# A hybrid decoder step on one core: differences kept in SBUF, per-layer stores moved to GpSimd

## The chip, the cores and the metric

The kernel runs on one core of a Trainium2 chip. The metric is the device time of one execution in microseconds. Before the change the median of three runs is 2677.23 us (2677.14 to 2685.69).

## The reference, cut to what matters

One decoder layer over 1024 prompt positions and 8 single-step samples, so 1032 columns (`NT`). Two branches (an SSD branch and a gated delta branch) are merged, then come an FFN and per-layer embeddings:

```python
h = _rms_norm(x, norm_mix)
proj = jnp.einsum('bld,de->ble', h, w_in)           # z, xbc, dt, qkv, gate, b, a, mgate
y, new_ssm = _ssd_chunked(...)                       # branch 1
o, new_gdn = _gated_delta_chunked(...)               # branch 2
o = _rms_norm(o, gdn_norm) * jax.nn.silu(gate)
mix = g_ssm * (y @ w_branch_ssm) + g_gdn * (o @ w_branch_gdn)
x = x + mix @ w_out
gt, up = jnp.split(_rms_norm(x, norm_ffn) @ w_ffn_in, 2, axis=-1)
x = x + (jax.nn.silu(gt) * up) @ w_ffn_out
pe = p @ w_pl_proj
x = x + pe * jax.nn.sigmoid(_rms_norm(x, norm_pl) @ w_pl_gate)
return _rms_norm(x, norm_final)
```

All data is float32 in DRAM. The kernel splits each operand into a high and a low part (`fp32r`), and takes three matmuls for a product: high by high, high by low, low by high.

## The kernel before, in words

Columns of x are features on 128 partitions in 8 blocks, rows are positions. The whole residual stays in SBUF as `x2` (also named `acc`). Matmul results lie in eight PSUM tiles of four pools: `pd` (3), `pt` (2), `py` (2), `pz` (1).

A scheduler orders the instructions of each engine by data and priority; weights are loaded by `load_w` with a high priority. `split_raw` splits a weight on ScalarE (`wh`, L138) and VectorE (`wl`, L139). All DMAs of the kernel before are issued from SyncE (`SPq` in rows), in the order in which the scheduler lists them, so a DMA that waits holds those listed behind it.

*The early stage.* `load_o` (L1085) brings the eight blocks of the delta branch: a block of `og_d` and one of the gate, silu on ScalarE, product on VectorE, then the split into `o` (`hilo`, L189 and L190). Blocks 0 to 3 take the two `lt` buffers, 4 to 7 the `op` slab tiles; all gate blocks share the two `sg` buffers. The per-layer inputs `pr` are loaded beside it and transposed into `ple`, which is stored to `ple_d` (L1111). The first two per-layer products `pe` follow, their copies out of PSUM on ScalarE (L1123). Then the eight blocks of the branch product with `o`; `residual` (L1153) loads a block of x into `xf` and transposes it into `x2`.

*The output product* runs in two halves of 516 columns. Behind the second half's blocks 4 to 7 the differences `t3` of two feature blocks are computed and stored to `t3_d` (L1248). Behind the first half, eight normalised tiles `n` are split into `b11` and `b21`, and stored to `n_d`. `roots` makes the inverse root `rb` (reciprocal, L1206).

*The late stage.* The FFN's first product uses a Strassen-like scheme of seven half-size products over row halves: tiles `b11`, `b21`, `bt1` to `bt4` and `b22` are its right sides (names in rows drop the digits: `bq` holds `b11`, `b21`, `bt2` and `bt3`; `t` is `t3`, `n` is `n1` and `n2`, `g`, `u`, `x` are sums). Before it, `per_layer_late` (L1128) makes the other six blocks of `pe` as fillers: 18 products of six matmuls over 344 columns, in six PSUM tiles in turn; ScalarE copies each (L1133) into one of five staging tiles (`x1`, two of `g1`, `u2`, `u3`), from which it is stored to `pe_d` (L1134). While TensorE does these, the block under `prep` reloads `t3` and `n` (L1308 to L1311), and makes the right sides on VectorE: L1318 multiplies `t3` by `rb`, L1319 and L1323 make sums and differences, `put` (L1224 and L1225) splits, L1228 scales again, L1327 makes the rows of `bt1`. Behind all of it stand the two first sums: `ffn_first(0)` and `ffn_first(1)`, each two products of 12 matmuls by two column halves over `b11` and `b21`; the second product's result is added by VectorE (L1284) into `g`. Then `ffn_in(0)` takes the other five products of row 0, each also by two column halves.

Of the kernel before, what the change touches and what calls it, by code (L numbers as in the profile page):

```python
# [8 lines left out]
F32 = mybir.dt.float32  # L9
# [7 lines left out]
P = 128  # L17
# [3 lines left out]
NB = 8  # L21
NT = NP + NB
# [17 lines left out]
def hybrid_step(  # L40
# [9 lines left out]
    V, S, G, TE = nc.vector, nc.scalar, nc.gpsimd, nc.tensor  # L50
    dma = nc.sync.dma_start
# [7 lines left out]
    dr = ctx.enter_context(tc.tile_pool(name="dr", bufs=1, space=DRAM))  # L59
# [12 lines left out]
    ident = cp.tile([P, P], F32, name="ident")  # L72
# [132 lines left out]
    with (  # L205
# [4 lines left out]
        for tt in range(9):  # L210
            n = P if tt < 8 else NB
# [8 lines left out]
        for g in range(3):  # L220
            t0, tn = PARTS[g]
            xns = []
            for tt in range(3 * g, 3 * g + 3):
                n, xt = (P if tt < 8 else NB), xts[tt]
# [7 lines left out]
            for k in range(KD):  # L232
                pool, name = ((pt, "pt"), (py, "py"), (pz, "pz"), (pt, "pt"), (py, "py"))[k % 5]
                t = pool.tile([P, 512], F32, name=name)
# [23 lines left out]
    pe_d = dr.tile([8, P, NT], F32, name="pe_d")  # L258
# [1 line left out]
    vb_d = dr.tile([8, P, NC, P], F32, name="vb_d")  # L260
    ple_d = dr.tile([2, P, 2, NT], F32, name="ple_d")
    n_d = dr.tile([8, P, NT // 2], F32, name="n_d")
    t3_d = dr.tile([4, P, NT // 2], F32, name="t3_d")
    bcd_d = dr.tile([2, 4, NB, P], F32, name="bcd_d")


# [49 lines left out]
    with tc.tile_pool(name="pr", bufs=1, side="right", reuse_waits="tile") as pr:  # L316
# [67 lines left out]
        for hh in range(2):  # L384
            q = slice(64 * hh, 64 * hh + 64)
# [3 lines left out]
        for src, dst in ((acum, colA), (dtb, colB), (q1, colQ)):  # L389
            for q in range(2):  # L390
                t = pt.tile([P, 512], F32, name="pt")
# [249 lines left out]
    with (  # L641
# [35 lines left out]
        def solves():  # L677
            for b4 in range(2):
                yield from solve(b4)
                yield  # L680
# [146 lines left out]
        last, side = None, solves()  # L827
# [248 lines left out]
    pM = ExitStack()  # L1076
    slb = pM.enter_context(tc.tile_pool(name="slb", bufs=8, reuse_waits="tile"))
    b2 = pM.enter_context(tc.tile_pool(name="b2", bufs=2, reuse_waits="tile"))

    def part_tile(name, dt=F32R):  # L1080
        return slb.tile([P, 2, NT], dt, name=name, tag="parts")

    ops = []

    def load_o(dst, k):  # L1085
        if k >= 4 and k % 2 == 0:
            ops.append(part_tile("op", F32))
        t = b2.tile([P, NT], F32, name="lt") if k < 4 else ops[-1][:, k % 2]
        dma(t[:, :NP], og_d[k])
        G.tensor_copy(t[:, NP:], odec[:, k])  # L1090
        gt = b2.tile([P, NT], F32, name="sg")
        dma(gt, gate_d[k])
        S.activation(gt, gt, AF.Silu)
        V.tensor_tensor(t, t, gt, ALU.mult)
        hilo(dst[:, 0, k % 4], dst[:, 1, k % 4], t)

    pacts = []
    for k in range(2):
        t = part_tile("ple")
        pacts.append((t[:, 0], t[:, 1], t))  # L1100
    for tt in range(9):
        n = P if tt < 8 else NB
        pr_ = b2.tile([P, 256], F32, name="pr", tag="xf")
        dma(pr_[:n], p_prompt[0, 0, tt * P : tt * P + P, :] if tt < 8 else p_sample[0, :, 0, :])
        t = pt.tile([P, 512], F32, name="pt")
        ts = slice(tt * P, tt * P + n)
        for k in range(2):
            TE.transpose(t[:, k * P : k * P + n], pr_[:n, k * P : k * P + P], ident[:n, :n])
            hilo(pacts[k][0][:, ts], pacts[k][1][:, ts], t[:, k * P : k * P + n])
# [18 lines left out]
    def per_layer_late(f, pacts, pools, rooms):  # L1128
        def ev(t0, tn, o):
            pool, name = rooms[0]  # L1130
            rooms.append(rooms.pop(0))
            t = pool.tile([P, NT // 2], F32, name=name, bufs=2 if name == "g1" else 1)
            S.copy(t[:, :tn], o)  # L1133
            dma(pe_d[f, :, t0 : t0 + tn], t[:, :tn])  # L1134

        dense(load_w(w_pl_proj[:, f * P : f * P + P], 2), pacts, ev, CHUNKS, pools)

# [13 lines left out]
    x2 = acc  # L1151

    def residual(f):  # L1153
        xf = b2.tile([P, 9, P], F32, name="xf")
        fs = slice(f * P, f * P + P)
        dma(xf[:, 0:8], x_prompt[0, :, fs].rearrange("(t p) d -> p t d", p=P))
        dma(xf[:NB, 8], x_sample[:, 0, fs])
        for q in range(3):
            t = pt.tile([P, 512], F32, name="pt")
            n = 4 if q < 2 else 1  # L1160
            w = P if q < 2 else NB
            for k in range(n):
                TE.transpose(t[:, k * P : k * P + w], xf[:w, 4 * q + k], ident[:w, :w])
            S.copy(x2[:, f, 512 * q : 512 * q + n * w], t[:, : n * w])

    macts = []
# [1 line left out]
    for f in range(8):  # L1168
# [4 lines left out]
        sg = sgp[f][:, 1] if f < 2 else b2.tile([P, NT], F32, name="sg")  # L1173
# [38 lines left out]
    QT = NT // 2  # L1212
# [10 lines left out]
    def put(q, k, src):  # L1223
        S.copy(q[:, 0, k], src)  # L1224
        V.tensor_tensor(q[:, 1, k], src, q[:, 0, k].bitcast(F32), ALU.subtract)  # L1225

    def scaled(dst, j, ts):
        V.scalar_tensor_tensor(dst, x2[:, j, ts], gain(G_FFN, j), rb[:, ts], ALU.mult, ALU.mult)  # L1228

    for hf in range(2):  # L1230
        parts = tuple((hf * QT + c * QC, QC) for c in range(2))
        for f in range(8):
            def ev(t0, tn, o):
                a = x2[:, f, t0 : t0 + tn]
                V.tensor_tensor(a, a, o, ALU.add)
                if f == 7:
                    squares(f, sqs, rb, t0, tn, b2)

            dense(load_w(w_out[:, f * P : f * P + P], 8), macts, ev, parts)
            if f < 7:  # L1240
                squares(f, sqs, rb, hf * QT, QT, b2)
            if hf == 1 and f >= 4:
                t3 = b2.tile([P, QT], F32, name="t3", tag="sg")
                S.activation(t3, x2[:, f - 4, HALF[1]], AF.Copy, scale=gain(G_FFN, f - 4))
                V.scalar_tensor_tensor(
                    t3, x2[:, f, HALF[1]], gain(G_FFN, f), t3, ALU.mult, ALU.subtract
                )
                dma(t3_d[f - 4], t3)  # L1248
        for t0, tn in parts:
            roots(sqs, rb, t0, tn)  # L1250
        if hf == 0:
            for k in range(4):
                for q, j in ((b11, k), (b21, k + 4)):
                    n = b2.tile([P, QT], F32, name="n", tag="sg")
                    scaled(n, j, HALF[0])
                    put(q, k, n)
                    dma(n_d[j], n)
# [28 lines left out]
    def gate_rows(i):  # L1286
        rg = wp.tile([P, 8, P], F32, name="wraw")
        dma(rg, w_ffn_in[:, i * P : i * P + P].rearrange("(k p) f -> p k f", p=P))
        return rg
# [3 lines left out]
    def ffn_first(i, rg):  # L1293

        x1 = sqs[:, HALF[0]] if i == 1 else ft.tile([P, QT], F32, name="x1")
        g1 = ft.tile([P, QT], F32, name="g1", bufs=2)
        with tc.high_priority(offset=2000):
            w11 = split_raw(rg[:, 0:4], 4)
        product(w11, b11, lambda ts, o: S.copy(x1[:, ts], o))
        with tc.high_priority(offset=2000):  # L1300
            w12 = split_raw(rg[:, 4:8], 4)
        product(w12, b21, plus(g1, x1))
        firsts[i] = x1, g1

    with tc.tile_pool(name="prep", bufs=4, side="right", reuse_waits="tile") as prep:
        t3s, n1s, n2s = ([prep.tile([P, QT], F32, name=n) for _ in range(4)] for n in ("t3", "n1", "n2"))
        for k in range(4):
            dma(t3s[k], t3_d[k])  # L1308
            dma(n1s[k], n_d[k])
        for k in range(4):  # L1310
            dma(n2s[k], n_d[k + 4])  # L1311
        fills = [(pd, "pd"), (py, "py"), (pd, "pd"), (py, "py"), (pd, "pd"), (pz, "pz")]
        rooms = [(ft, "x1"), (ft, "g1"), (ft, "u2"), (ft, "g1"), (ft, "u3")]
        for f in range(EARLY, 8):
            per_layer_late(f, pacts, fills, rooms)
        for k in range(4):
            t3, n1 = t3s[k], n1s[k]
            V.tensor_tensor(t3, t3, rb[:, HALF[1]], ALU.mult)  # L1318
            V.tensor_tensor(n1, n1, t3, ALU.add)  # L1319
            put(bt2, k, n1)  # L1320
            put(bt3, k, t3)
        for k in range(4):
            V.tensor_tensor(n2s[k], n2s[k], n1s[k], ALU.subtract)  # L1323
            put(bt4, k, n2s[k])
        for k in range(4):
            scaled(t3s[k], k + 4, HALF[1])
            V.tensor_tensor(n1s[k], t3s[k], n1s[k], ALU.subtract)  # L1327
            put(bt1, k, n1s[k])
        for k in range(4):
            put(b22, k, t3s[k])  # L1330
        with tc.high_priority(offset=2000):
            early = [gate_rows(0), gate_rows(1)]
        for i in range(2):
            ffn_first(i, early[i])

    gp = ctx.enter_context(tc.tile_pool(name="gp", bufs=3, side="right", reuse_waits="tile"))
    gacts = {}
# [63 lines left out]
    b2 = ctx.enter_context(tc.tile_pool(name="b3", bufs=2, reuse_waits="tile"))  # L1401
    rb2 = slb.tile([P, NT], F32, name="rb2", bufs=1)
    sqs2 = slb.tile([P, NT], F32, name="sqs2", bufs=1)
    h3acts, _ = half_slabs("h3")
# [66 lines left out]
    for part in (PARTS[:2], PARTS[2:]):  # L1471
        for f in range(8):
            if len(gws) == f:
                pool, tag = (slb, "parts") if f < 4 else (gp, "gu") if f < 7 else (nrm, "rs")
                w = pool.tile([P, 2, 8, P], F32R, name="gw", tag=tag)
# [47 lines left out]
```

## Time and profile before

| | |
|---|---|
| median of three runs | 2677.23 us |
| the profiled execution | 2679.42 us, its span 2677.6 us |
| TensorE matmuls (PE) in flight | 2588.4 us, 97% of the span |
| VectorE (DVE) busy | 1780.0 us, 66% |
| ScalarE (ACT) busy | 1117.0 us, 42% |
| GpSimd (POOL) busy | 251.4 us, 9% |

Busy shares are means over stages with different limits. Times in the rows are counted from the span's start. A wait stands with the engine that waited, its line, and what ended the wait. A matmul's shown duration overlaps the next one's, so the distance of starts is what one costs.

### The profile page before, as it was taken

Reading aid. Unit: us, or ns where it says so; the run is one execution under the profiler, and the core shown is the slowest. Engines: PE = TensorE matmul, PEld = TensorE weight load, DVE = VectorE, ACT = ScalarE, POOL = GpSimd, SP = SyncE. Lnnn points to the kernel's source line nnn. Section 1 sums busy time; section 2 is a strip of 40 time slices with the busy share of each in tenths; the row PEclk is TensorE's granted clock in tenths of the full one; section 3 lists DMA queues with packets and bytes.
Section 4 is the critical chain, followed back from the end, with each engine's and each line's share of the span. In section 5 each row is a group of like instructions: output and inputs, shape, how many; then the busy total and the mean of one; then the engine's idle time right before and its main releaser. Section 6 shows DMA issues by size and latency. Waiting matters only on the chain. (4 is left out here: it accounts for less than half of the span.)

```text
span 2677.6 us, 46492 instructions
## 1 busy us (share of the span) xinstructions
PE 2588.4 (97%) x18167; PEld 2503.8 (94%) x18167; DVE 1780.0 (66%) x3325; ACT 1117.0 (42%) x2322; POOL 251.4 (9%) x495
## 2 busy tenths in 40 slices
PE   7999999999999999999999999998999999999998
PEld 7999999989989989898999988998999999999998
DVE  6677897588557666574455566456777767677665
ACT  6555545455365373342332234344322222222443
POOL 0111222121120110210010000010000000000010
PEclk9999999999999999999999999998999999999999
DMA  4355445555353453357674447535111111121122
GB/s 124 117 156 170 135 158 145 116 119 160 102 126 117 115 138 113 106 167 216 185 220 138 120 142 247 163 120 190 59 51 50 48 48 48 50 61 45 50 87 95
DMA packets 473673, 322.33 MB, mean 120 GB/s; under 512 B 45425, under 2 KB 443930, under 8 KB 472174
## 3 DMA queue, kind: packets, MB, share of 16 engines
q1 hardware_dynamic: 471054, 310.94, 40.2%
q10 hardware_dynamic: 2400, 8.42, 0.8%
q8 instruction: 143, 2.34, 0.3%
q14 instruction: 76, 0.62, 0.1%
HBM read 237.70 MB, written 81.60 MB: 119 GB/s over the span
## 5 line engine op out<-in xcount | busy, mean ns | idle before, releaser
L69 PE MATMUL pd<-h,wh 128*128 128x344 f32 x4272 | 1042.9, 326 | 17.6 <-ACT wh L138 10.2
L69 PEld LDWEIGHTS pd<-h,wh 128*128 128x128 f32 x4272 | 741.8, 190 | 30.1 <-ACT wh L138 12.3
L69 PE MATMUL pd<-h,wl 128*128 128x344 f32 x2136 | 692.8, 324 | 2.1 <-DVE wl L139 1.2
L139 DVE TENSOR_TENSOR wl<-wraw,wh 128x512 fp32r<-128x512 f32 (+1 forms) x362 | 251.1, 695 | 277.6 <-ACT wh L138 269.5
L138 ACT CAST wh<-wraw 128x512 fp32r<-128x512 f32 (+1 forms) x362 | 221.1, 613 | 483.6 <-PE pd L69 328.5
L69 PEld LDWEIGHTS pd<-h,wl 128*128 128x128 f32 x2136 | 404.9, 190 | 7.2 <-DVE wl L139 5.5
L69 PE MATMUL pd<-gu,wh 128*128 128x344 f32 (+2 forms) x1056 | 248.6, 319 | 0.0
L69 PE MATMUL pd<-y,wh 128*128 128x344 f32 x768 | 186.5, 324 | 0.0
L69 PEld LDWEIGHTS pd<-gu,wh 128*128 128x128 f32 x1056 | 182.3, 188 | 0.0
L69 PE MATMUL pd<-gu,wl 128*128 128x344 f32 (+2 forms) x528 | 169.2, 320 | 0.0
L715 ACT ACTIVATE ab<-ab,ncolA 128x128 f32<-128x128 f32 x256 | 81.8, 391 | 138.9 <-POOL ab L711 138.8
L1390 DVE TENSOR_TENSOR acc<-acc,pd 128x344 f32<-128x344 f32 x216 | 109.5, 510 | 44.4 <-PE pd L69 40.1
L69 PEld LDWEIGHTS pd<-y,wh 128*128 128x128 f32 x768 | 132.5, 188 | 1.2 <-issue 0.2
L428 ACT COPY raw<-pd 128x344 f32<-128x344 f32 x144 | 62.6, 438 | 151.4 <-PE pd L69 138.9
L69 PE MATMUL pd<-y,wl 128*128 128x344 f32 x384 | 124.5, 325 | 0.0
L69 PE MATMUL pd<-bq,wh 128*128 128x258 f32 (+1 forms) x572 | 108.7, 286 | 0.0
L69 PEld LDWEIGHTS pd<-gu,wl 128*128 128x128 f32 x528 | 99.2, 188 | 0.0
L69 PE MATMUL pd<-o,wh 128*128 128x344 f32 x384 | 94.9, 330 | 3.6 <-DVE o L190 3.3
L442 DVE SCALAR_TENSOR_TENSOR ca<-raw,cwm,ca 128x1056 f32<-128x1056 f32 x72 | 95.9, 1332 | 2.0
L442 DVE SCALAR_TENSOR_TENSOR ca<-raw,cwg,ca 128x1056 f32<-128x1056 f32 x72 | 96.5, 1341 | 0.8
L69 PE MATMUL pd<-h,gw 128*128 128x384 f32 (+1 forms) x576 | 94.6, 323 | 0.0
L69 PE MATMUL pd<-mx,wh 128*128 128x258 f32 x512 | 92.8, 283 | 0.0
(524 smaller groups left out, 5135.8 us busy)
## 6 DMA issues: line engine op xcount, KB each, us to landing
wraw<-in_w_in_dram SPq DMA_DIRECT2D x88, 512.0 KB
ab<-acum_d SPq DMA_DIRECT2D x32, 512.0 KB
out_dram<-sd SPq DMA_DIRECT2D x48, 256.0 KB
wraw<-in_w_ffn_in_dram SPq DMA_DIRECT2D x24, 512.0 KB
ru<-in_w_ffn_in_dram SPq DMA_DIRECT2D x22, 512.0 KB
wro<-in_w_ffn_out_dram SPq DMA_DIRECT2D x72, 128.0 KB
sg_d<-mg SPq DMA_DIRECT2D x16, 516.0 KB
bb<-rk_d SPq DMA_DIRECT2D x8, 1024.0 KB
```

The source lines that it names most:

```text
L69: TE.matmul(o, l, r, start=start, stop=stop)
L138: S.copy(wh[:, :n], raw[:, k0 : k0 + n])
L139: V.tensor_tensor(wl[:, :n], raw[:, k0 : k0 + n], wh[:, :n].bitcast(F32), ALU.subtract)
L428: S.copy(raw[:, 3 + t0 : 3 + t0 + n], o[:, :n])
L442: V.scalar_tensor_tensor(ca, raw[:, j : j + CONVN], w[j], ca, ALU.mult, ALU.add)
L715: S.activation(ab[:, h], ab[:, h], AF.Exp, bias=ncolA[:, c, h0 + h : h0 + h + 1])
L1390: V.tensor_tensor(a, a, o, ALU.add)
```

## The change

- The four differences `t3` are no longer stored and reloaded. They are made as two tiles in the pool `bx`, whose buffers the residual's `xf` tiles had, and stay there until the last split. The pool lies on the other side of SBUF and is closed after the first sums. The residual's sample rows get a small tile `xs`.
- The per-layer input tiles `pr` take this pool too.
- Gate blocks 4 and 5 get a slab tile `gt` of their own.
- The 18 stores of `per_layer_late` are issued from GpSimd's queue.
- `ffn_first(0)` stands ahead of the last two preparation loops, `ffn_first(1)` between them. The early `gate_rows` come before both.
- With the reloads of `t3` gone, the loads of `n` are listed earlier.

```diff
-    t3_d = dr.tile([4, P, NT // 2], F32, name="t3_d")
...
+    pX = ExitStack()
+    bx = pX.enter_context(tc.tile_pool(name="bx", bufs=2, side="right", reuse_waits="tile"))
...
+        if k == 4:
+            gts.append(part_tile("gt", F32))
...
-        gt = b2.tile([P, NT], F32, name="sg")
+        gt = gts[0][:, k % 2] if k in (4, 5) else b2.tile([P, NT], F32, name="sg")
...
-        pr_ = b2.tile([P, 256], F32, name="pr", tag="xf")
+        pr_ = bx.tile([P, 256], F32, name="pr", tag="xf")
...
-            dma(pe_d[f, :, t0 : t0 + tn], t[:, :tn])
+            G.dma_start(pe_d[f, :, t0 : t0 + tn], t[:, :tn])
...
-        xf = b2.tile([P, 9, P], F32, name="xf")
+        xf = bx.tile([P, 8, P], F32, name="xf")
+        xs = b2.tile([NB, P], F32, name="xs")
...
-                t3 = b2.tile([P, QT], F32, name="t3", tag="sg")
+                if f % 2 == 0:
+                    t3x = bx.tile([P, 2, QT], F32, name="t3", tag="xf")
+                t3 = t3x[:, f % 2]
+                t3s.append(t3)
...
-                dma(t3_d[f - 4], t3)
...
-            dma(t3s[k], t3_d[k])
...
+        with tc.high_priority(offset=2000):
+            early = [gate_rows(0), gate_rows(1)]
+        ffn_first(0, early[0])
         for k in range(4):
             scaled(t3s[k], k + 4, HALF[1])
             V.tensor_tensor(n1s[k], t3s[k], n1s[k], ALU.subtract)
             put(bt1, k, n1s[k])
+        ffn_first(1, early[1])
         for k in range(4):
             put(b22, k, t3s[k])
-        with tc.high_priority(offset=2000):
-            early = [gate_rows(0), gate_rows(1)]
-        for i in range(2):
-            ffn_first(i, early[i])
+    pX.close()
```

The scheduler's order follows. On ScalarE, from the fourth to the seventh copy of the late per-layer products (`x`, `g`, `u` are the staging tiles), before:

```order
L1133 COPY g_19089<-py 128x344
L1133 COPY u_19099<-pd 128x344
L138 CAST wh<-wraw 128x256
L1224 CAST bq_17886<-n_19020 128x516
L1224 CAST bq_17886<-n_19021 128x516
L1224 CAST bq_17886<-n_19022 128x516
L1224 CAST bq_17886<-n_19023 128x516
L1224 CAST bt_19011<-n_19024 128x516
L1224 CAST bt_19011<-n_19025 128x516
L1133 COPY x_19109<-pz 128x344
L1133 COPY g_19125<-pd 128x344
```

and now:

```order
L1136 COPY g_19084<-py 128x344
L1136 COPY u_19094<-pd 128x344
L1228 CAST bq_17895<-n_19019 128x516
L138 CAST wh<-wraw 128x256
L1136 COPY x_19104<-pz 128x344
L1228 CAST bq_17895<-n_19020 128x516
L1136 COPY g_19120<-pd 128x344
```

Six splits of `n` stood between the fifth and the sixth copy; now one does, and copies and splits alternate.

On VectorE, where the first sum `g` is added, before:

```order
L1327 TENSOR_TENSOR n_19023<-t_19019,n_19023 128x516
L1225 TENSOR_TENSOR b_19012<-t_19016,b_19012 128x516
L1225 TENSOR_TENSOR b_19012<-t_19017,b_19012 128x516
L1225 TENSOR_TENSOR bt_19010<-n_19023,bt_19010 128x516
L1225 TENSOR_TENSOR b_19012<-t_19018,b_19012 128x516
L1225 TENSOR_TENSOR b_19012<-t_19019,b_19012 128x516
L1284 TENSOR_TENSOR g_19321<-x_19320,pd 128x258
L1284 TENSOR_TENSOR g_19321<-x_19320,py 128x258
L1284 TENSOR_TENSOR g_19386<-rs,pt 128x258 x2
```

and now:

```order
L1229 TENSOR_TENSOR bt_19014<-n_19026,bt_19014 128x516
L1291 TENSOR_TENSOR g_19292<-x_19291,pd 128x258
L1291 TENSOR_TENSOR g_19292<-x_19291,py 128x258
L1336 TENSOR_TENSOR n_19019<-t_18788,n_19019 128x516
L1232 SCALAR_TENSOR_TENSOR t_18788<-acc,gcols,rs 128x516
L139 TENSOR_TENSOR wl<-s_19455,wh 128x512
L1229 TENSOR_TENSOR bt_19013<-n_19019,bt_19013 128x516
```

Row 0's `g` was behind the last split of `b22` (`b`) and of `bt1`; now it is ahead of all of `bt1`'s (`bt_19013`). Row 1's `g` (`g_19373`) stands between `bt1`'s splits, not shown.

On SyncE, in the early stage, from the second per-layer weight to the last gate load, before:

```order
L1089 DMA lt<-og_d 128x1024
L146 DMA wraw<-in_w_branch_gdn_dram 128x8x128
L1104 DMA pr<-in_p_sample_dram 8x256
L1089 DMA lt<-og_d 128x1024
L1092 DMA sg<-gate_d 128x1032
L1089 DMA op<-og_d 128x1024
L146 DMA wraw<-in_w_branch_gdn_dram 128x8x128
L1111 DMA ple_d<-ple 128x2064 x2
L146 DMA wraw<-in_w_branch_gdn_dram 128x8x128
L1092 DMA sg<-gate_d 128x1032 x2
L1089 DMA op<-og_d 128x1024
L1126 DMA pe_d<-pe 128x1032
```

and now:

```order
L1095 DMA gt<-gate_d 128x1032
L1114 DMA ple_d<-ple 128x2064
L146 DMA wraw<-in_w_branch_gdn_dram 128x8x128
L1114 DMA ple_d<-ple 128x2064
L146 DMA wraw<-in_w_branch_gdn_dram 128x8x128
L1092 DMA lt<-og_d 128x1024 x2
L1095 DMA sg<-gate_d 128x1032
L1092 DMA op<-og_d 128x1024
L146 DMA wraw<-in_w_branch_gdn_dram 128x8x128
L1095 DMA sg<-gate_d 128x1032
L1092 DMA op<-og_d 128x1024
L1095 DMA sg<-gate_d 128x1032
```

The loads of `og` 2 and 3 (`lt`) stood ahead of the two stores of `ple`; now they stand behind them, with the last three gate loads.

## Rows read from the trace of the kernel before

**Rows 1.** TensorE's longest waits, 1300 to 1950; line, then releaser: us, times, longest

```profile
PE pz L69 <- ACT x L1133: 11.9, 1, 11.9
...
PE pd L69 <- DVE g L1284: 4.2, 1, 4.2
...
PE pd L69 <- DVE o L190: 3.3, 1, 3.3
...
PE pt L1163 <- DMA xf<-in_x_prompt_dram: 1.9, 1, 1.9
```

**Rows 2.** Stretches: us, busy and instructions by engine, granted clock, DMA share, GB/s

```profile
1852.00:1856.00 4.00, 1.36 (x5) 1.36 (x6) 4.00 (x8) 2.72 (x6) 0.00 (x0) 0.50 0.66 227
...
1868.00:1872.00 4.00, 4.00 (x36) 4.00 (x35) 4.00 (x7) 2.28 (x5) 0.00 (x0) 1.00 0.44 131
...
1884.00:1888.00 4.00, 3.12 (x14) 3.13 (x15) 2.82 (x8) 0.64 (x1) 0.00 (x0) 0.50 0.00 0
```

**Rows 3.** TensorE's timeline: start, us, engine line operation, idle before and releaser

```profile
1831.96 0.67 PE L69 MATMUL pd<-bq,wh 128*128 128x344 f32 x2
...
1841.62 0.48 PE L69 MATMUL pd<-bq,wh 128*128 128x344 f32 x2
...
1854.64 0.94 PE L69 MATMUL pz<-bq,wh 128*128 128x344 f32 x2 [11.91 <-ACT x L1133]
...
1884.88 0.80 PE L69 MATMUL pd<-bt,wh 128*128 128x258 f32 x2 [4.17 <-DVE g L1284]
...
1894.29 0.40 PE L69 MATMUL py<-b,wh 128*128 128x258 f32 x2
...
1895.72 0.40 PE L69 MATMUL pd<-bq,wh 128*128 128x258 f32 x2
```

**Rows 4.** SyncE's timeline of DMA issues

```profile
1825.76 1.03 SPq L146 DMA_DIRECT2D wraw<-in_w_pl_proj_dram  x2
...
1844.89 3.65 SPq L1311 DMA_DIRECT2D n<-n_d  x4
...
1848.86 0.32 SPq L1134 DMA_DIRECT2D pe_d<-x  x1
...
1862.37 0.66 SPq L1134 DMA_DIRECT2D pe_d<-x  x1
```

**Rows 5.** Waits of all engines, 1830 to 1895

```profile
ACT bq L1224 <- DVE n L1319: 9.3, 4, 3.7
...
DVE wl L139 <- ACT wh L138: 4.8, 5, 2.4
```

**Rows 6.** VectorE's timeline

```profile
1831.99 3.39 DVE L1206 RECIPROCAL rs<-rs 128x258 f32<-128x258 f32 x2
...
1840.53 0.70 DVE L1318 TENSOR_TENSOR t<-t,rs 128x516 f32<-128x516 f32 x1 [1.79 <-DMA t<-t_d]
...
1871.59 0.68 DVE L139 TENSOR_TENSOR wl<-wraw,wh 128x512 fp32r<-128x512 f32 x1
...
1872.19 0.69 DVE L1225 TENSOR_TENSOR bt<-n,bt 128x516 fp32r<-128x516 f32 x1
...
1884.41 0.41 DVE L1284 TENSOR_TENSOR g<-x,pd 128x258 f32<-128x258 f32 x1
```

**Rows 7.** Stretches of the early stage

```profile
1630.00:1650.00 20.00, 14.40 (x63) 13.31 (x63) 13.77 (x15) 13.76 (x16) 0.00 (x0) 0.74 1.01 345
...
1650.00:1670.00 20.00, 20.00 (x131) 19.77 (x129) 10.46 (x14) 7.25 (x10) 0.00 (x0) 1.00 0.25 75
```

**Rows 8.** Waits of SyncE's queue, 1575 to 1660

```profile
SPq L1092 <- DVE op L1094: 5.5, 1, 5.5
```

**Rows 9.** ScalarE's timeline

```profile
1854.14 0.45 ACT L1133 COPY x<-pz 128x344 f32<-128x344 f32 x1
...
1866.97 0.38 ACT L1299 COPY x<-pd 128x258 f32<-128x258 f32 x1 [0.97 <-DMA pe_d<-x]
```

**Rows 10.** GpSimd by form: line operation, count, busy us, mean ns, idle before

```profile
L1197 POOL TENSOR_TENSOR rs<-rs,sqt 128x516 f32<-128x516 f32 x12 | 16.3, 1361 | 207.5 <-ACT sqt L1196 207.5
```

More of the change, by code (lines that the diff above doesn't have):

```diff
@@ L1078, in hybrid_step @@
     b2 = pM.enter_context(tc.tile_pool(name="b2", bufs=2, reuse_waits="tile"))
+    pX = ExitStack()
+    bx = pX.enter_context(tc.tile_pool(name="bx", bufs=2, side="right", reuse_waits="tile"))
     def part_tile(name, dt=F32R):
         return slb.tile([P, 2, NT], dt, name=name, tag="parts")
-    ops = []
+    ops, gts = [], []
     def load_o(dst, k):
@@ L1153, in residual @@
     def residual(f):
-        xf = b2.tile([P, 9, P], F32, name="xf")
+        xf = bx.tile([P, 8, P], F32, name="xf")
+        xs = b2.tile([NB, P], F32, name="xs")
         fs = slice(f * P, f * P + P)
-        dma(xf[:, 0:8], x_prompt[0, :, fs].rearrange("(t p) d -> p t d", p=P))
-        dma(xf[:NB, 8], x_sample[:, 0, fs])
+        dma(xf, x_prompt[0, :, fs].rearrange("(t p) d -> p t d", p=P))
+        dma(xs, x_sample[:, 0, fs])
         for q in range(3):
@@ L1162, in residual @@
             for k in range(n):
-                TE.transpose(t[:, k * P : k * P + w], xf[:w, 4 * q + k], ident[:w, :w])
+                TE.transpose(t[:, k * P : k * P + w], xf[:, 4 * q + k] if q < 2 else xs, ident[:w, :w])
             S.copy(x2[:, f, 512 * q : 512 * q + n * w], t[:, : n * w])
@@ L1228, in scaled @@
         V.scalar_tensor_tensor(dst, x2[:, j, ts], gain(G_FFN, j), rb[:, ts], ALU.mult, ALU.mult)
+    t3s = []
     for hf in range(2):
@@ L1305, in hybrid_step @@
     with tc.tile_pool(name="prep", bufs=4, side="right", reuse_waits="tile") as prep:
-        t3s, n1s, n2s = ([prep.tile([P, QT], F32, name=n) for _ in range(4)] for n in ("t3", "n1", "n2"))
+        n1s, n2s = ([prep.tile([P, QT], F32, name=n) for _ in range(4)] for n in ("n1", "n2"))
         for k in range(4):
-            dma(t3s[k], t3_d[k])
             dma(n1s[k], n_d[k])
```

## The prediction, made before the changed kernel ran

> **What bounds the kernel now.** I read the page first: TensorE has matmuls in flight nearly throughout, so a gain can only come from the places where it stands still or runs slowly. The list of its waits then says where: around the change there are four large ones, 11.9, 4.2, 3.3 and 1.9 us [rows 1]. The table by stretches adds what a wait costs behind its end: after the 11.9 us and after the 4.2 us hole the granted clock is 0.50, the lower level of 1.2 GHz, and a stretch of 4 us holds 5 or 14 matmuls instead of 36 [rows 2]. Last, the timelines of each engine say which work was late.
>
> *The late stage.* The late per-layer products begin at 1831.96; the eleventh begins at 1841.62, so one takes 0.97 us. After it TensorE stops until 1854.64, and again until 1884.88 [rows 3]. Eleven is five staging tiles plus six PSUM tiles: the sixth copy out of PSUM needs a staging tile whose store has landed. That store is queued on SyncE behind the reload of the differences (`t`) and of eight normalised tiles (`n`), and is issued only at 1848.86 [rows 4]. The sixth copy is also queued on ScalarE behind splits that wait 9.3 us in all for VectorE [rows 5], and VectorE itself stands behind the reload: its first product with `t` starts at 1840.53 after a wait on that DMA, 5.1 us after the reciprocal ended (1831.99 + 3.39 = 1835.38) [rows 6]. From there VectorE is the late engine: the second hole ends with its sum `g`, at 1884.41, queued behind all preparation [rows 6].
>
> Eighteen late products (18 x 0.97 = 17.4 us), the eight products of the two first sums and the ten of row 0 (18 x 1.43 = 25.7; one runs from 1894.29 to 1895.72 [rows 3]) follow each other without a gap if nothing is late: 1831.96 + 43.1 = 1875.1. In the trace they end at 1895.72. So 20.6 us is all that this stage can give back.
>
> *The early stage.* Between 1630 and 1650 there are 63 matmuls, in the 20 us behind them 131, at clocks of 0.74 and 1.00 [rows 7]. At 20 / 131 = 0.153 us each, 68 missing ones are 10.4 us. The DMA engines are full there (share 1.01) and SyncE waited 5.5 us before it could issue a gate load, for a buffer that VectorE was still reading [rows 7, 8].
>
> **The change part by part.**
> *Differences kept on chip.* Four stores and four reloads of 258 KB go, and with them the wait at VectorE's start. Nothing is computed more or less.
> *Normalised rows earlier.* On SyncE the first four loads of `n` now stand behind the third per-layer weight, ahead of the 512 KB weights of the FFN. Before, the second and third weight were issued from 1825.76 on [rows 4], 9 us before the reciprocal's end, so I count them as landed by 1835.4.
> *First sums moved up.* The sum of row 0 now stands ahead of the last two preparation loops on VectorE, that of row 1 between their rows. No work goes; it no longer stands last.
> I add up VectorE's new list from the reciprocal to the last split of `bt1`: 54 full operations at 0.60 us (starts 1871.59 and 1872.19 [rows 6]) = 32.4, six short ones (four sums out of PSUM, two half-width weight splits) at 0.35 = 2.1, so 34.5 us. For its waits on ScalarE I take the 4.8 us that it spent on `wh` before [rows 5]. That gives 1835.4 + 34.5 + 4.8 = 1874.7. Then come five more operations (3.0) and the sum that frees the PSUM tile of the last two products (0.4): 1878.1, and those two products take 2.9: 1881.0. TensorE, unhindered, would be there at 1875.1, so VectorE is the bound and 5.9 us of small holes stay in place of the large ones. The gain is 1895.7 - 1881.0 = 14.7 us. I charge 1 us for sums that VectorE then still owes.
>
> *Stores from GpSimd.* The trace has no DMA issued from GpSimd, so its price is unknown. Let c be the time by which one store follows another on that queue. From below: SyncE issues such a store in 0.32 us [rows 4]. From above: a store of `x` issued at 1862.37 is seen landed at 1866.97, 4.6 us [rows 4, 9]; that is c if GpSimd starts nothing before the last one is home. The nearest row of the engine itself is its sum over 128x516, 1.36 us [rows 10]; a store of 128x344 moves two thirds of that, and I take c = 1.2. The first late copy, no longer behind a weight split, ends at 1831.96 + 0.97 + 0.45 [rows 3, 9], say 1833.5. The copy that opens the first sum needs the sixteenth store landed: 1833.5 + 16c + 4.6. It is due at about 1856.7, since the weight splits behind it on ScalarE feed the seventh product (1831.96 + 17.4 + 6 x 1.43 = 1857.9) and two operations of 0.6 lie between. So the stores cost 16c - 18.6 us: 0.6 at 1.2, nothing at 0.32, 55 at 4.6. GpSimd has nothing else to do here: its twelve sums of squares are over before the first store.
>
> The Trainium skill speaks against this part (DMA: Bandwidth & Descriptors, section on the anatomy of a DMA on the GpSimd path): about 2.0 us per DMA plus its bytes over 436 GB/s. By that a store of 172 KB is 2.4 us, as an estimate; if they ran strictly one by one the stores would cost 20 us and the change would lose. The page also says that most of those 2 us is the wait for the write's receipt, which can overlap. No row here shows which of the two holds.
>
> *Early stage.* Gate loads 4 and 5 get a tile of their own, and the prompt rows come through a separate pool, earlier. That takes away SyncE's 5.5 us wait, of which TensorE saw 3.3. Against it: the loads of `og` 2 and 3 now stand behind two stores of 1,032 KB in full queues, and the fourth to sixth early per-layer copy stand on ScalarE between splits that need those loads. 2 x 1,032 KB at 345 GB/s is 6 us. Bounds: 10.4 gained, 6 lost; I take 2.5 gained, the 3.3 less a little for the pieces that come later. The change of slab tiles costs nothing: a merged tile's first user comes more than ten products after the last reader.
>
> Sum: 14.7 - 1.0 - 0.6 + 2.5 = 15.6 us. The profiled execution took 2679.4 (span 2677.6); less 15.6 that is 2663.8. It lies 2.2 above the median of 2677.2, so I predict 2662 for the median.
>
> **The rivals.**
> *A, the store queue takes the place of the reload queue (slower).* GpSimd needs c over 2.2 us a store: then 16c - 18.6 exceeds the rest of the gain (16.2), ScalarE stands at the first sum's copy, behind it the weight splits, and TensorE waits for them. For it speaks that each store has 128 rows to describe and that five staging tiles bind copy and store; against it that the engine's own operations over 128 partitions take around 1.4 us. At c = 3.0, between 1.36 and 4.6, the stores cost 29.4: 2677.2 - 16.2 + 29.4 = 2690.
> *B, VectorE begins no earlier.* If the `n` loads land as late as `t` did (1840.5), everything behind moves by 5.1 and the gain is 10.5; with waits on ScalarE twice as long (its copies now wait for stores) 5.7. That is 2667 to 2672; I write 2670. For it: copies and splits alternate on ScalarE now.
> *C, all holes close.* 20.6 and half of 10.4 to all of it: 2646 to 2652. Against it: VectorE's 34.5 us and its waits do not fit into the 34.0 us until TensorE would take `bt1` (1831.96 + 17.4 + 14 x 1.43 = 1869.4).
> *D, the early stage gets worse* by up to 6: 2677.2 - 13.1 + 6 = 2670.
> *E, c near 2 us*: the stores cost 13.4 and 2674 comes out.
>
> **How the numbers follow.** Forecast (2657 to 2668) 0.45, C 0.12, B 0.18, D 0.10, E 0.05, A 0.10. A measurement of this kernel tells 0.3% (8 us) from no change, so faster is below 2669.2: the forecast, C, half of B and a third of D, 0.70. Within 0.3%: the rest of B and D, and E, 0.20. Slower, above 2685.3: A, 0.10. The range runs from 2654, where stores at no cost, half of VectorE's waits and two thirds of the early loss meet (2677.2 - 13.7 - 2.4 - 7), to 2678, at c just over 2; C and A stay outside.
>
> **What would show it.** Right: no wait of more than 3 us of TensorE at the late per-layer products; a single small wait on VectorE at the sums `u` or at `bt`; VectorE's first product with `t` at the reciprocal's end; the ten products of row 0 ending 43 to 50 us after the late products began instead of 63.8. GpSimd's stores follow each other at 0.9 to 1.4 us. Wrong on the stores: ScalarE's copies wait for DMA by several us each and the first sum's copy is the longest. Wrong on the early stage: TensorE's wait there ends on `og` 2 or 3 or on the early copies and is longer than 3.3 us. The forecast as a whole is wrong if the stage from the late products to row 0's end shrinks by less than 8 us.

## The result, and the profile after

The changed kernel takes 2662.87 us (median of five runs, 2661.04 to 2668.10), the kernel before 2678.76 us (five runs beside it, 2677.14 to 2685.69). The ratio is 0.9938, 95% interval 0.9918 to 0.9959: faster by 0.4 to 0.8%. When it ran again the ratio was 0.9927 (0.9913 to 0.9941). 2662 was forecast.

The profiled execution has a span of 2665.8 us. It and a second profile of the same kernel are cut here at five places of TensorE's timeline, in us:

| stretch, by what TensorE does | before | after | after, second profile |
|---|---|---|---|
| start to the first early per-layer product | 1617.19 | 1621.09 | 1610.79 |
| from there to the first output product | 115.27 | 111.51 | 109.98 |
| output product, to the first late per-layer product | 99.50 | 101.56 | 101.23 |
| late stage, to the end of row 0's ten products | 63.76 | 49.79 | 49.85 |
| the rest | 781.88 | 781.85 | 781.75 |

The first row is spread between executions: in the fourteen profiles of this study it lies from 1610.8 to 1621.1, with a mean of 1617.1 in the three kernels without the new pool and 1617.7 in the eleven that have it. What the change moves is in the next three rows: -3.8, +2.1 and -14.0 us, in sum -15.7 (in the second profile -17.5), against 15.6 forecast. The first row varies by 10 us from one execution to the next, so that the median came out within 1 us of 2662 is in part luck.

TensorE's waits between 1300 and 1950, as line, releaser, total, times, longest. The holes of 11.9, 4.2, 3.3 and 1.9 us [rows 1] are gone; no single one is over 2.2 us:

```profile
...
PE pd L69 <- DVE wl L139: 2.2, 2, 1.9
PE pd L69 <- DVE sgp L1182: 2.2, 1, 2.2
PE pd L69 <- DVE u L1291: 1.6, 1, 1.6
...
PE pt L69 <- DVE g L1291: 1.2, 1, 1.2
...
PE pt L69 <- ACT bt L1228: 1.1, 1, 1.1
PE pd L69 <- ACT pe L1126: 1.0, 1, 1.0
...
```

TensorE's timeline in the late stage. The late products run without a gap from 1834.16 to the first sum at 1851.39 (17.2 us; 17.4 was counted). Three small waits follow, on VectorE's sums and on `bt`:

```profile
1834.16 0.66 PE L69 MATMUL pd<-bq,wh 128*128 128x344 f32 x2
...
1851.39 0.40 PE L69 MATMUL pd<-bq,wh 128*128 128x258 f32 x2
...
1873.15 0.48 PE L69 MATMUL pt<-bt,wh 128*128 128x258 f32 x2 [1.22 <-DVE g L1291]
...
1875.52 1.48 PE L69 MATMUL pt<-bt,wh 128*128 128x258 f32 x4 [1.07 <-ACT bt L1228]
...
1880.97 0.51 PE L69 MATMUL pd<-b,wh 128*128 128x258 f32 x2 [1.62 <-DVE u L1291]
```

VectorE: its first product with `t` starts at 1838.01, behind the reciprocal and one short split; the last split of `bt1` at 1875.67. SyncE issued the first five loads of `n` from 1829.71 on, ahead of the FFN's weights. The other three came behind two of these (`ru`), the last two at 1839.06; all eight stand ahead of the four 512 KB weights (`wraw`) issued from 1841.48 on:

```profile
1834.19 3.39 DVE L1210 RECIPROCAL rs<-rs 128x258 f32<-128x258 f32 x2
1837.66 0.42 DVE L139 TENSOR_TENSOR wl<-wraw,wh 128x256 fp32r<-128x256 f32 x1
1838.01 1.29 DVE L1324 TENSOR_TENSOR t<-t,rs 128x516 f32<-128x516 f32 x2
...
1875.67 0.69 DVE L1229 TENSOR_TENSOR bt<-n,bt 128x516 fp32r<-128x516 f32 x1
```

```profile
1829.71 1.76 SPq L1315 DMA_DIRECT2D n<-n_d  x4
...
1839.06 1.07 SPq L1317 DMA_DIRECT2D n<-n_d  x2
```

GpSimd's stores, first the timeline (start, time on the engine), then the median from issue to landing. The shortest distance is 0.81 us (1838.27 to 1839.08, not shown). The 18 stores take from 1836.27 to 1856.07, so 1.16 us each on average; they follow ScalarE's copies, so this is no limit of GpSimd's:

```profile
1836.27 0.70 POOL L1137 DMA_DIRECT2D pe_d<-x  x1 [6.58 <-ACT x L1136]
...
1853.81 0.54 POOL L1137 DMA_DIRECT2D pe_d<-x  x1 [0.32 <-issue]
1854.68 0.54 POOL L1137 DMA_DIRECT2D pe_d<-g  x1 [0.33 <-issue]
1856.07 0.54 POOL L1137 DMA_DIRECT2D pe_d<-u  x1 [0.85 <-ACT u L1136]
```

```profile
pe_d<-g POOLq DMA_DIRECT2D x7, 172.0 KB, 4.8
pe_d<-u POOLq DMA_DIRECT2D x7, 172.0 KB, 4.0
```

ScalarE's copies waited for a store to land five times, 3.2 us in all and 1.02 at most; at the late products TensorE did not stop for it. The last of these waits is that of the copy that opens the first sum:

```profile
1857.82 0.38 ACT L1306 COPY x<-pd 128x258 f32<-128x258 f32 x1 [0.60 <-DMA pe_d<-x]
```

Stretches (us, busy and instructions of PE, PEld, DVE, ACT, POOL, clock, DMA share, GB/s). In the early stage 94 matmuls stand where there were 63 [rows 7]; it begins 3.9 us later here, and at the same distance from its start there are 96. In the output product (0.83) and behind the wait on `bt` (0.60) the clock is a mean of time at 2.4 GHz and at 1.2 GHz; both are taken up below:

```profile
1630.00:1650.00 20.00, 17.08 (x94) 15.91 (x93) 14.23 (x16) 11.48 (x12) 0.00 (x0) 0.91 1.02 356
...
1800.00:1810.00 10.00, 8.07 (x56) 7.86 (x55) 5.90 (x11) 5.37 (x10) 2.60 (x2) 0.83 0.49 153
...
1876.00:1880.00 4.00, 3.26 (x14) 2.67 (x13) 2.89 (x6) 1.14 (x2) 0.00 (x0) 0.60 0.35 100
```

### The profile page after: what moved, and what is told of

It reads as the page before. It is cut to its first block, busy times and chain, and to the rows that moved or that the text cites. A ratio compares the mean times of both kernels' runs of the same rounds, so it can differ in the third digit from the quotient of the medians.

```text
span 2665.8 us, 46476 instructions
## 1 busy us (share of the span) xinstructions
PE 2585.8 (97%) x18167; PEld 2500.3 (94%) x18167; DVE 1781.4 (67%) x3329; ACT 1115.3 (42%) x2318; POOL 261.3 (10%) x513
## 4 chain that ended last, share of the span: by engine, by line
PE 48%; DVE 2%; DMA 2%; ACT 0%; issue 0%; DVEq 0%; SPq 0%; ACTq 0%
PE pd L69 33%; PE py L69 6%; PE pt L69 5%; PE pz L69 2%; DMA kg<-ktok_d 0%; DMA n_d<-n 0%; PE pt L1167 0%; DVE wl L139 0%; DMA pr<-in_p_prompt_dram 0%; DMA sg<-gate_d 0%; PE pt L973 0%; DVE y L190 0%; DMA mg<-y_d 0%; DVE xo L1474 0%; DMA wraw<-in_w_ffn_in_dram 0%
```

## The experiments

Since executions differ by some us ahead of the change, the length of a stage in the trace decides and the time only supports it. In two profiles of the changed kernel the late stage differs by 0.06 us. The first kernels, with the parts each has (p: pairs on chip and `n` early; m: sums moved up; s: stores from GpSimd; g: gate blocks 4 and 5 apart), and the stretches in us; the ratio is to the kernel before, run beside them:

| kernel | parts | to the first output product | output product | late stage | ratio (95%) |
|---|---|---|---|---|---|
| before | none | 115.27 | 99.50 | 63.76 | 1 |
| after_again | p m s g | 109.98 | 101.23 | 49.85 | 0.9927 (0.9913 to 0.9941) |
| stores_sp | p m g | 110.71 | 101.48 | 49.96 | 0.9945 (0.9931 to 0.9958) |
| sums_last | p s g | 110.02 | 101.21 | 53.82 | 0.9952 (0.9937 to 0.9966) |
| pairs_dram | m s g | 111.40 | 102.15 | 61.38 | 0.9982 (0.9971 to 0.9992) |
| gate_shared | p m s | 115.69 | 99.41 | 50.67 | 0.9944 (0.9925 to 0.9962) |
| b_pairs_chip | p | 115.24 | 99.96 | 55.00 | 0.9963 (0.9952 to 0.9974) |
| b_sums_up | m | 113.91 | 99.28 | 60.02 | 0.9972 (0.9962 to 0.9983) |
| b_stores_pool | s | 114.95 | 101.13 | 63.63 | 1.0000 (0.9987 to 1.0013) |

**The yardstick** (after_again: no edit).

> The changed kernel once more, as the yardstick for the other kernels of this call. The stage from the first late per-layer product to the end of row 0's ten products took 63.8 us before and 49.8 us in the first profile of the changed kernel. The first per-layer product of the early stage stood at 1617.2 us before and at 1621.1 us now, although nothing ahead of it was edited except where the prompt rows and gate blocks are loaded. If that shift comes from the change, it is there again at about +3.9 us; if it is the spread between executions of the work ahead, this profile shows another value, and the whole execution moves with it. Expected ratio 0.994.

The late stage came out again to 0.06 us, the start did not (1610.79): the +3.9 us of the first profile is spread between executions.

**Stores back on SyncE** (stores_sp).

```diff
-            G.dma_start(pe_d[f, :, t0 : t0 + tn], t[:, :tn])
+            dma(pe_d[f, :, t0 : t0 + tn], t[:, :tn])
```

> The changed kernel with the 18 late per-layer stores back on SyncE. Theory (the stores must leave SyncE's queue): they stand behind the loads of the normalised rows and between the 512 KB weight loads, which wait for their buffers; ScalarE's copies wait for staging tiles, TensorE gets a hole of 3 to 8 us at the sixth to tenth late product and half clock behind it, the stage grows from 49.8 to 54 to 60 us, and the time is 5 to 10 us above the changed kernel's. Rival (without the reload of the differences the queue is short enough): the stage stays under 52 us and the time within 2 us of the changed kernel's.

The rival was right on the stage: 49.96 us. TensorE's waits from 1830 to 1900 in this kernel show that the late products do wait for staging tiles, 1.5 us, and take 19.7 us instead of 17.2:

```profile
PE pt L69 <- DVE g L1291: 2.2, 1, 2.2
PE pd L69 <- DVE u L1291: 1.7, 1, 1.7
PE py L69 <- ACT u L1136: 1.5, 2, 1.3
```

The end does not move by it: in both kernels TensorE's last wait of the stage ends on VectorE's sum `u`, 46.8 us behind the first late product in the changed kernel and 47.0 here. TensorE's waits behind the products are 3.9 us in both. What the changed kernel gains at the products it loses at the lower clock behind its waits (0.60 from 1876 to 1880); in stores_sp the granted clock is 1.00 throughout the stage. VectorE works up to `u` without a wait here. In the changed kernel a split of row 1's weights stands ahead of `u` and waits 1.1 us for ScalarE, which itself waits 2.7 us for TensorE:

```profile
1879.24 0.62 ACT L138 CAST wh<-s 128x512 fp32r<-128x512 f32 x1 [2.72 <-PE pt L69]
1879.89 0.69 DVE L139 TENSOR_TENSOR wl<-s,wh 128x512 fp32r<-128x512 f32 x1 [1.11 <-ACT wh L138]
```

The rival's other half, a time within 2 us, is not seen: the medians are 2663.87 and 2658.15 us. But the three stretches differ by 1.1 us in all and the intervals of the two ratios overlap, so the times do not show a difference of the kernels.

**Sums behind all preparation** (sums_last; the same lines as at the end of the diff of the change, turned back).

```diff
-        ffn_first(0, early[0])
...
-        ffn_first(1, early[1])
...
             put(b22, k, t3s[k])
+        for i in range(2):
+            ffn_first(i, early[i])
```

> The changed kernel with both first sums listed behind all preparation again. Theory: VectorE is the bound of the stage, so its sum g, which frees the PSUM tiles, comes after the last split again; TensorE waits 4 us there and runs at half clock behind it, the stage is 54 to 57 us instead of 49.8, the time 4 to 7 us above the changed kernel's. Rival (the place of the sums costs nothing, since VectorE's list has the same length either way and the last split decides): under 2 us.

4.0 us longer, in one hole of 6.8 us on `g`; the theory's mechanism, just under its range of 54 to 57. The granted clock behind the hole is 0.50:

```profile
PE pd L69 <- DVE g L1291: 6.8, 1, 6.8
```

**Pairs through DRAM** (pairs_dram).

```diff
-                if f % 2 == 0:
-                    t3x = bx.tile([P, 2, QT], F32, name="t3", tag="xf")
-                t3 = t3x[:, f % 2]
+                t3 = b2.tile([P, QT], F32, name="t3", tag="sg")
...
+                dma(t3_d[f - 4], t3)
...
+            dma(t3s[k], t3_d[k])
```

> The changed kernel with the four differences stored to DRAM and reloaded again, all else kept (stores from GpSimd, sums moved, early stage). Theory: VectorE's first product with t starts 3 to 5 us later, since the reload stands behind the last store and ahead of or between the normalised rows, and VectorE is the bound: the stage is 53 to 56 us, the time 3 to 6 us above the changed kernel's. Rival (the stores of the late products were all that the reload delayed): under 1.5 us.

The direction was right, the size was not: 11.5 us. VectorE's first product with `t` starts 5.6 us behind the reciprocal's end, 5.2 us later than in the changed kernel, where 3 to 5 were expected; the rest comes behind it. SyncE's timeline in this kernel: a 512 KB weight is listed ahead of three loads of `n` and waits for its buffer until 1853.16, and they with it:

```profile
1843.96 0.50 SPq L1318 DMA_DIRECT2D n<-n_d  x1
1853.16 0.38 SPq L1295 DMA_DIRECT2D wraw<-in_w_ffn_in_dram  x1
1853.59 1.64 SPq L1318 DMA_DIRECT2D n<-n_d  x3
```

VectorE's differences of those rows follow 34.1 us behind the first late product; in the changed kernel the first one stands 12.4 us behind it (1846.51):

```profile
1864.28 1.90 DVE L1330 TENSOR_TENSOR n<-n,n 128x516 f32<-128x516 f32 x3
```

**One part alone, on the kernel before.** The edits are those of the change's diff, each by itself; b_pairs_chip has the pool `bx` with it, for `pr` and `xf` too, and the early loads of `n`.

> The kernel before with one part alone: the pair differences stay on chip (with the pool that they need, the loads of the normalised rows listed early by it), stores from SyncE, sums last, gate blocks in the shared buffers. In the runs so far the stage from the first late product to the end of row 0 takes 63.8 us before, 49.8 with all parts, 61.4 with all parts but this one, 50.0 with all but the stores and 53.8 with all but the moved sums. Theory (the reload is the root; the normalised rows behind it and the stores are late by it): this part alone gives 53 to 56 us. Rival (each part is needed, since the stores of the late products still stand behind 512 KB weight loads): 58 us or more.

> The kernel before with the first sums listed ahead of the last preparation loops, nothing else. Theory: the 11.9 us hole stays, the 4.2 us hole goes, as in the step between 53.8 and 49.8 us with the other parts: stage 59 to 61 us, 3 to 5 us of the time. Rival (behind the large hole VectorE has caught up or is so late that its place costs nothing): stage 63 to 64 us.

> The kernel before with the late stores from GpSimd alone. Theory: the 11.9 us hole of TensorE goes, but VectorE is the bound, begins no earlier and stands behind the reloads, so the time comes back as waits at the sums: stage 61 to 65 us, the time within 3 us of the kernel before. Rival (the hole is the loss, and it goes): stage 53 us or less, the time 9 to 11 us below the kernel before.

All three theories held for the stage: 55.00, 60.02 and 63.63 us. (The time of b_sums_up, 6.9 us lower by the medians, fell by more than the 3 to 5 us expected and than the 3.7 us of the stage.) The stores alone take the 11.9 us hole away and give nothing. TensorE's waits of that kernel from 1830 to 1900: the time is back at the sum `g`, where it was 4.2 us, and at copies and splits:

```profile
PE pd L69 <- DVE g L1284: 9.5, 1, 9.5
PE pz L69 <- ACT g L1133: 1.8, 1, 1.8
PE pz L69 <- ACT bt L1224: 1.4, 1, 1.4
...
```

Its SyncE has the order seen in pairs_dram: with the stores out of the list, the weight stands ahead of three `n` loads and holds them from 1847.6 to 1855.7. VectorE's first product with `t` starts 6.1 us behind the reciprocal's end there (not shown), against 5.1 before [rows 6]. So the largest hole of the profile was not the largest loss.

This kernel also shows how fast GpSimd can issue stores. Where several copies lie ready, one store follows another at 0.53 us:

```profile
1840.15 0.54 POOL L1134 DMA_DIRECT2D pe_d<-u  x1
1840.68 0.54 POOL L1134 DMA_DIRECT2D pe_d<-g  x1
```

**Gate blocks in the shared buffers** (gate_shared).

```diff
-        gt = gts[0][:, k % 2] if k in (4, 5) else b2.tile([P, NT], F32, name="sg")
+        gt = b2.tile([P, NT], F32, name="sg")
```

> The changed kernel with gate blocks 4 and 5 back in the two shared buffers. From the first early per-layer product to the first output product it takes 115.3 us before and 110.0 to 111.5 in five profiles with the gate tile. Theory (SyncE's 5.5 us wait for the buffer came to TensorE as a 3.3 us hole and half clock): 114 to 116 us again, the time 3 to 5 us above the changed kernel's. Rival (the separate pool for the prompt rows and the other order of loads did it): 110 to 112 us.

The time of the early stage came as the theory said, 115.69 us, but not in its way. SyncE's wait for the `op` block is 3.2 us instead of 5.5, and the granted clock from 1630 to 1650 is 0.91, as in the changed kernel. TensorE's waits from 1615 to 1730 are eight, all on splits of the branch blocks, 7.3 us in all and 2.0 at most. In the changed kernel they are 3.7 us in all: 2.2 on `sgp`, 1.0 on `pe`, 0.5 on `o`.

```profile
PE pd L69 <- ACT o L189: 3.4, 3, 1.6
PE pd L69 <- DVE o L189: 2.0, 1, 2.0
PE pd L69 <- DVE o L190: 1.9, 4, 0.5
```

The output product behind it takes 99.41 us, so over both stretches the tile gives 2.0 to 3.9 us; the ratios, whose intervals overlap, do not show it.

**Is VectorE's list the bound?** Three kernels are to take four operations, 2.4 us, off it ahead of the last split of `bt1`.

The first moves the weight sums of row 1 to GpSimd (w_pool; the other three sums likewise):

```diff
+        W = G if i == 1 else V
...
-            V.tensor_tensor(s3, a11, a21, ALU.subtract)
+            W.tensor_tensor(s3, a11, a21, ALU.subtract)
```

> The changed kernel with the four weight sums of the FFN's row 1 (lines 1354, 1355, 1359, 1362) on GpSimd, which has been idle since its last store. In the changed kernel VectorE does them between 1865.8 and 1871.4 us, ahead of the last splits of bt1. Theory (VectorE's list sets the end of the stage): four operations of 0.60 us less, so 2.4 us, and with them part of the half clock behind the last holes: stage 46 to 47.5 us instead of 49.8, tail unchanged at 781.8. Rival (the holes come from the chain of difference, copy and split of each block through ScalarE, not from the length of VectorE's list): stage 49.3 to 50 us. Other rival: row 1's weights come too late from GpSimd, and the tail grows by as much.

The second moves the differences of `bt1` there (sub_pool):

```diff
-            V.tensor_tensor(n1s[k], t3s[k], n1s[k], ALU.subtract)
+            G.tensor_tensor(n1s[k], t3s[k], n1s[k], ALU.subtract)
```

> The changed kernel with the four differences of bt1 (line 1336) on GpSimd. The same 2.4 us leave VectorE's list, but each difference takes about 1.4 us on GpSimd instead of 0.69. Theory (VectorE's list is the bound): stage 46.5 to 48.5 us. Rival (the chain through the difference, ScalarE's copy and the split is the bound): 50 to 52 us, since each link is 0.7 us longer.

The third lists row 1's weight sums, and their splits, later on VectorE (weights_later):

```diff
-        with tc.high_priority(offset=2000):
+        with tc.high_priority(offset=100 if i == 1 else 2000):
```

> The changed kernel with the four weight sums of row 1 listed later on VectorE (a lower priority), behind the last splits of bt1 and b22. Nothing goes to GpSimd. With them on GpSimd the stage was 50.4 us, and VectorE's operations beside GpSimd's took 1.75 us instead of 0.7. Theory (VectorE's list up to the last split of bt1 sets the end): 2.4 us less ahead of that split, so the holes at bt1 (1.2 and 1.1 us, with half clock behind) shrink and the stage is 46 to 48 us instead of 49.8, the tail 781.8 as before, the time 2 to 3.5 us below the changed kernel's. Rival (the chain through ScalarE's copies of each block is the bound): 49.3 to 50.2 us. Other rival: the splits of row 1's weights come too late behind them, and the tail grows to 783 us or more.

On GpSimd both missed: 50.42 us each, slower than the changed kernel's stage; ratios 0.9945 (0.9928 to 0.9962) and 0.9935 (0.9918 to 0.9953). In w_pool this is outside both rivals (the tail is 781.8 us). In sub_pool it lies in the rival's 50 to 52 us, but the traces of both kernels show something that no rival named: VectorE itself became slower. In w_pool GpSimd's timeline is

```profile
1861.05 2.29 POOL L1354 TENSOR_TENSOR s<-wraw,ru 128x512 f32<-128x512 f32 x1 [8.83 <-DVE wl L139]
1863.42 1.62 POOL L1355 TENSOR_TENSOR ru<-ru 128x512 f32<-128x512 f32 x1
1865.12 1.60 POOL L1359 TENSOR_TENSOR wraw<-ru,wraw 128x512 f32<-128x512 f32 x1
1866.80 1.60 POOL L1362 TENSOR_TENSOR wraw<-wraw 128x512 f32<-128x512 f32 x1
```

and beside it VectorE's:

```profile
1861.49 0.69 DVE L1336 TENSOR_TENSOR n<-t,n 128x516 f32<-128x516 f32 x1
1862.10 3.49 DVE L1232 SCALAR_TENSOR_TENSOR t<-acc,gcols,rs 128x516 f32<-128x516 f32 x2
1865.52 1.75 DVE L1336 TENSOR_TENSOR n<-t,n 128x516 f32<-128x516 f32 x1
1867.19 1.75 DVE L139 TENSOR_TENSOR wl<-ru,wh 128x512 fp32r<-128x512 f32 x1
1868.87 1.29 DVE L1229 TENSOR_TENSOR bt<-n,bt 128x516 fp32r<-128x516 f32 x2
```

Four operations of VectorE take 1.75 us each there, and 0.65 each (x2 in 1.29) right behind it: some 4.2 us lost to save 2.4. In sub_pool, too, four operations of VectorE beside GpSimd's take 1.65 to 1.79 us. So these two kernels did not shorten VectorE's list and do not test the theory.

Listing row 1's sums later on VectorE gives 47.23 us, in the theory's range. Between the reciprocal and the last split of `bt1` VectorE then has 48 full operations instead of 54, since a weight split and a split of `b22` have moved behind it too. That is 3.6 us less work, at 1.4 us more of waits, and that split ends 2.3 us earlier. The split of row 1's weights that waited 1.1 us ahead of `u` also stands behind `u` now, so the gain is not that of the shorter list alone; no run separates the two. TensorE's waits from 1830 to 1900 are

```profile
PE pd L69 <- DVE u L1291: 1.3, 1, 1.3
PE pd L69 <- ACT wh L138: 0.7, 1, 0.7
PE pt L69 <- DVE wl L139: 0.5, 1, 0.5
PE pd L69 <- DVE wl L139: 0.4, 1, 0.4
```

with the clock at 1.00 throughout. The rival, a chain through ScalarE's copies, is also answered by the changed kernel's trace, where ScalarE stands still for VectorE's differences, three times ahead of its part of a split of `bt1`, 2.5 us at most:

```profile
1872.03 0.62 ACT L1228 CAST bt<-n 128x516 fp32r<-128x516 f32 x1 [2.48 <-DVE n L1336]
```

The tail grows from 781.85 to 782.27 us, so some 2.1 us stay. The ratio is 0.9920 (0.9906 to 0.9933), the lowest of the study; its interval overlaps that of after_again, so the kernel as a whole is not shown to be faster than the changed one, only its stage.

**Four buffers for the normalised tiles** (n_four).

```diff
-                    n = b2.tile([P, QT], F32, name="n", tag="sg")
+                    n = b2.tile([P, QT], F32, name="n", tag="sg" if q is b11 else "lt")
```

> The changed kernel with the eight normalised tiles in four buffers (those of the gate blocks and of the branch blocks in turn) instead of two. From the first output product to the first late product it took 99.3 to 100.0 us in four profiles and 101.1 to 102.2 in six; in all of them VectorE waits 1.5 to 2.9 us for a store of such a tile to land, and TensorE 1.5 to 2.5 us for the weight split behind it; where it is the longer time the granted clock of the next 10 us is 0.83 or 0.84 instead of 1.00. Theory: with four buffers that wait goes, the stretch is 97.5 to 98.5 us in any execution, and the time 1.5 to 3.5 us below the changed kernel's. Rival (the split waits for ScalarE or the reciprocal in any case): 99.3 us or more.

Neither came: the waits for stores are gone and the output product takes 105.30 us (the late stage 48.96; ratio 0.9955, 0.9939 to 0.9970). VectorE, no longer held up, does the rest of the eight tiles ahead of the sums that free TensorE's PSUM tiles:

```profile
PE pd L69 <- DVE acc L1240: 6.3, 1, 6.3
```

The shortage of buffers had kept the order. So the 2 us that the output product lost are not won back, and why it is longer in most kernels is only seen, not tested: TensorE's wait on the split `wl` there is 1.5 us in before and b_sums_up and 1.8 to 2.5 in the other eleven profiles, and in eight of these the mean clock of the 10 us at it or behind it is 0.83 or 0.84.

## Why the prediction was right

*What bounds the late stage.* It said VectorE, with small holes of TensorE as its mark; three came, of 1.2, 1.1 and 1.6 us, where one was named. Leaving stores on SyncE costs the products 2.4 us and the stage 0.1 to 0.2; with row 1's sums and splits listed later on VectorE it is 2.6 us shorter. Putting the sums last makes it 4.0 us longer. So it is shown that VectorE's order sets the end. Its length is not all: of the 2.6 us, up to 1.1 can be the wait ahead of `u`, which nothing in the prediction named. With it, `u` began 4.2 us behind the last split of `bt1` (1876.28 to 1880.50), where five operations in 3.0 us were forecast; the five are there.

*VectorE's start.* Forecast: the differences on chip and early `n` loads let it begin at the reciprocal's end. It began 0.4 us behind it (5.1 before [rows 6]).

*VectorE's list.* Forecast 34.5 us of work and 4.8 of waits, 39.3 from the reciprocal to the last split of `bt1`; it took 38.7 (1837.58 to 1876.28), of which 35.9 busy and 2.8 idle. The 54 full operations are there, and seven short ones instead of six. Two errors of 1.4 and 2.0 us nearly cancelled, which is luck. The stage fell by 14.0 us; 14.7 less 0.6 for the stores was forecast, and the 1 us charged for a backlog behind it did not come (tail 781.85 against 781.88).

*The stores.* c was taken as 1.2 us, which is the pace at which the copies came (1.16). GpSimd's own distance is at most 0.81 us in the changed kernel and 0.53 in b_stores_pool; the formula then gives no cost, and the copy that opens the first sum waited 0.60 us. So rivals A and E fall. The estimate of 2.4 us per such store by the Trainium skill (DMA: Bandwidth & Descriptors, anatomy of a DMA on the GpSimd path) is no distance here. The page lays most of the fixed 2 us to the wait for the write's receipt, and the trace agrees: little of a store's time is the queue's. Stores follow at 0.53 us and land, in the changed kernel, 4.0 to 4.8 us (medians) after issue. The prediction laid the 11.9 us hole to the store queue and to VectorE's lateness at once and priced the stores as a cost alone. The runs tell the two apart: the queue made the hole, yet its removal alone is worth 0.1 us, since VectorE behind the same reload is as late. With the other parts in place the stores' move gives the stage no more than 0.2 us. What removes the loss is the part that keeps the pairs on chip and pulls the `n` loads ahead (8.8 us alone, 11.6 between pairs_dram and the changed kernel), then the moved sums (3.7 alone, 4.0 with the rest). No run separates the pairs on chip from the early `n` loads.

*The early stage.* 2.5 us was taken, from the 3.3 us hole. The gate tile is worth 4.1 to 5.7 us to the first output product (115.69 in gate_shared; 109.98 to 111.58 in the nine profiles with it; 113.91 to 115.27 in the other four without it). Against the kernel before, 3.8 and 5.3 us were gained in the two profiles, and TensorE's waits there fell by only 1.8 (5.5 to 3.7). The rest lies in the clock as far as the profiles tell, 0.74 before [rows 7] and 0.91 after: it was in the bound of 10.4 and should have been priced in part. The output product then gave 1.7 to 2.1 back, which nothing in the prediction named; with 1.7 and 3.6 us net in the two profiles the term came near by two misses of opposite sign, which is luck. Of rival D (the loads of `og` behind the stores of `ple`) the early copies show a wait of 1.0 us on `pe`; the 2.2 us on `sgp` stand behind ScalarE's list, and no run traces them to `og`. Both together are less than was gained.

*Rivals B and C.* B's late begin did not come. C failed where it said: 38.7 us of VectorE do not fit into its 34.0; three holes and a stretch at clock 0.60 remain.

## What to carry to other kernels

The largest wait in the list names what is late last, not what it is worth: before a queue is relieved, ask which engine behind the wait would be just as late, and sum that engine's whole list. A store or load taken out of an in-order queue changes the order of what is left; look at which loads now stand behind one that waits for its buffer. More buffers or an idle engine are not free either: the first may let work pass that should wait, the second may slow the engine it relieves.

## What the runs showed of the hardware

GpSimd's elementwise work does not run beside VectorE's here. While GpSimd did sums of two SBUF tiles (1.60 us each), VectorE's operations on two SBUF tiles took 1.75 us instead of 0.65 to 0.75, and one of each went in turn (in w_pool VectorE's start at 1865.52 and 1867.19, GpSimd's at 1865.12 and 1866.80). Where one of VectorE's was under way first, GpSimd's took 2.29 us (1861.05). The Trainium skill (SBUF — State Buffer, SBUF: two separate sides) says that the two share a port pair as an exclusive lock for such operands; the trace agrees. GpSimd's DMA issues, 0.54 us each, left VectorE's operations beside them at 0.69 us; stores of 172 KB followed each other at as little as 0.53 us (b_stores_pool).

A wait of TensorE of about 2 us amid dense work was followed by a mean clock of 0.83 over 10 us in some executions, so by some time at 1.2 GHz, and by 1.00 (2.4 GHz) in others: 1.9 us by the lower one (the changed kernel), 2.4 us by the full one (b_pairs_chip, 1800 to 1810). The runs do not show what decides it.
